# Seven block products in place of eight in the input projections of a two-layer encoder's feed-forwards

## The chip, the core and the metric

The kernel runs on one core of a Trainium2 chip. Its time is the device time of one execution in microseconds (us), and the figure for a kernel is the median of several executions. Engines are named as in the profile: PE multiplies matrices, PEld loads its weights, DVE, ACT and POOL are the vector, scalar and general engines, SP issues the DMAs.

## What is computed

A trunk of two layers runs over 576 tokens: a prompt of 512 and a sample of 64, which share all weights. Each layer is a feed-forward, a token mixer, and another feed-forward; so there are four feed-forwards. The change touches nothing but these. Cut to what matters, one is

```
def _swiglu(h, w_in, w_out):
    gate, up = jnp.split(h @ w_in, 2, axis=-1)      # w_in: 1024 x 5632
    return (jax.nn.silu(gate) * up) @ w_out         # w_out: 2816 x 1024

for l in range(DEPTH):                              # DEPTH = 2
    mod = (cond @ ada_w[l] + ada_b[l]).reshape(b, N_SUB, 3, D_MODEL)
    shift, scale, gate = mod[:, :, 0], mod[:, :, 1], mod[:, :, 2]
    hh = _modulated_norm(x, norm_g[l, 0], shift[:, 0], scale[:, 0])
    x = x + 0.5 * gate[:, 0, None] * _swiglu(hh, ff_w_in[l, 0], ff_w_out[l, 0])
    ...                                             # mixer, then the second feed-forward
```

Everything is float32. The vectors shift, scale and gate come from `cond @ ada_w`, nine products of 1024 x 1024 for each layer.

## The kernel before

**Layout.** Features lie in partitions, tokens along the free dimension. The 1024 features of the input are eight tiles of 128 (index k), and the tokens are two halves of 288. A float32 operand is held as two tiles in a rounded type: `XH`, the rounded value, and `XL`, what is left. A product of two operands is three matmuls (wh by XH, wh by XL, wl by XH), each a 128 x 128 weight against 288 columns, summed in one PSUM bank.

**Feed-forward** (`ffn`, line 638). The 2816 inner features are 22 column tiles. For each there is a pair of weight blocks, one of gate columns and one of up columns, each of eight 128 x 128 tiles (1024 columns in SBUF). `dense` (line 379) multiplies a pair: for each token half, gate over all k, then up over all k; 2 halves x 2 tiles x 8 k x 3 = 96 matmuls. After gate, ACT takes silu out of PSUM into `sg`; after up, DVE multiplies `sg` by the PSUM bank into `hm`, ACT rounds it into `HH`, DVE writes the rest into `HL`. The 22 tiles come in three chunks of 8, 8 and 6; after each chunk its share of the output projection is multiplied from `HH` and `HL` and added to the residual `x`. The first two pairs are multiplied together (`start_sub`, line 629; `dense_first`, line 431, in the first feed-forward), with their first token half running while the norm of the second half is still being worked out.

**Weights.** `w_dma` (line 354) fetches blocks of 512 KB by SP's queue into a ring of three buffers (`stage`). `w_prep` (line 364) splits one: ACT copies it rounded into `wh`, DVE subtracts that into `wl`; `wh` and `wl` are rings of four. During a pair the two blocks of the next pair are split.

**PSUM.** Two rings of four banks, `d` for the dense products and `a` for all else.

**Background work.** `ada_task` (line 585) works out shift, scale and gate on DVE while the feed-forwards run: for each of 136 weight tiles two operations of 1024 columns (`jk`). A planner (`Model`, `Sched`, lines 113 to 286) keeps rough times of each engine while the program is built, and puts a step of a background task into the instruction stream when its due time has come on PE's clock; the due times of `ada_task` are 5.6 us apart in the first feed-forward and 8.5 us in the next two. `finish` (line 278) builds a task to its end before anything else is built. The planner only sets the order in which instructions are written; each engine then works through its own list in that order.

All instructions are issued through one helper, so that nearly all rows carry line 188; operations are told apart by tile names.

Of the kernel before, what the change touches and what calls it, by code (L numbers as in the profile page):

```python
# [45 lines left out]
DSH = ((2, 4, 6), (1, 4, 6))  # L46


def plan():
    """The weight tiles in the order in which they are used, as pairs of blocks of up to eight 128 x 128 products;  # L50
    a tile is (source, index, rows, column)."""
# [6 lines left out]
    def ffn(f):  # L58
        for j0, nj in CHUNKS:
            for j in range(j0, j0 + nj):  # L60
                two([("in", f, tuple(range(8)), j * P), ("in", f, tuple(range(8)), FF + j * P)])
            ks = tuple(range(j0, j0 + nj))
            for ms in outs(nj):
                two([("out", f, ks, m * P) for m in ms])
# [40 lines left out]
def outs(nk):  # L105
    """The output tiles of each pair of blocks whose sums run over nk products."""
# [4 lines left out]
class Model:  # L111
    """Rough times of the engines, in ns, by which the background work is interleaved with the dense products."""
# [37 lines left out]
    def free(self, key, bufs):  # L150
        """When the ring's next buffer is free."""
# [73 lines left out]
class Ring:  # L225
    """A tile pool whose reuse of buffers the model sees."""
# [15 lines left out]
class Sched:  # L242
    """Interleaves the background work with the stream of dense products."""
# [45 lines left out]
def encoder_step(ctx: ExitStack, tc: tile.TileContext, a, o):  # L289
# [30 lines left out]
    # ---------------------------------------------------------------- constants  # L320
# [26 lines left out]
    # ---------------------------------------------------------------- weights  # L347
# [15 lines left out]

    def w_prep(i, g, E=None):
        if i >= len(pairs) or g >= len(pairs[i]):
            return
# [12 lines left out]
    def dense(evacs, ks=None, inter=False, mid=None):  # L379
        """The output tiles of a pair of blocks, or of two pairs, for the first half of the tokens, then for the  # L380
        second; evac(g, half, psum) for tile g of a pair."""
# [48 lines left out]

    def dense_first(evacs, feed):
        """The first two pairs of all, step by step for both halves as feed makes their inputs."""
# [36 lines left out]
    # ---------------------------------------------------------------- rsqrt, norms  # L469
# [23 lines left out]
    def norm_r(pool, halves):  # L493
        """1/rms of each token of these halves, tokens in partitions."""
# [61 lines left out]
    # ---------------------------------------------------------------- adaLN vectors  # L556
# [48 lines left out]
    # ---------------------------------------------------------------- the last products of a sub-layer  # L605
# [1022 lines left out]
```

## Time and profile before

| | |
|---|---|
| median of 3 runs | 2508.98 us (2506.79 to 2511.66) |
| profiled execution, first to last instruction | 2512.2 us; its time is listed as this span alone |
| PE busy | 2430.6 us, 97% |
| DVE busy | 1506.0 us, 60% |
| ACT busy | 835.3 us, 33% |
| POOL busy | 354.2 us, 14% |
| mean granted TensorE clock | 0.972 of full speed |

A row of the page's part 5 or of a grouped listing reads: line, engine, operation, output tile <- input tiles, shapes, count | busy us, mean ns of one | idle time of the engine before them and what ended it. PE's matmuls overlap, so their summed duration exceeds the span; the time that one takes from the stream is read from the chain of waits, which lists stretches of work with their number of instructions. A timeline row reads: start us, duration us, engine, line, operation, tiles, count, and in brackets how long the engine was idle before and who released it.

### The profile page before, as it was taken

The page shows a single profiled execution, that of the slowest core. Times are in us where ns is not written, and L with a number is a line of the kernel's source. Part 1 is how long each engine was busy: PE and PEld are TensorE (multiplying, and loading weights), DVE is VectorE, ACT ScalarE, POOL GpSimd, SP SyncE. Part 2 cuts the span into 40 slices and gives each one's busy share as a digit, 9 for nine tenths or more (in the row PEclk, how much of TensorE's full clock was granted, in tenths as well). Part 3 has the DMA queues.
Part 4 walks back from the last instruction along what each step waited for, and adds up shares of the span by engine and source line. Part 5 has one row for each costly group of instructions (what it writes and reads, how often), then busy time and mean ns, then how long its engine had stood idle before and what let it go on. Part 6 is the DMA issues. An engine that isn't in the chain of part 4 may idle for free.

```text
span 2512.2 us, 46274 instructions
## 1 busy us (share of the span) xinstructions
PE 2430.6 (97%) x19084; PEld 2357.9 (94%) x19084; DVE 1506.0 (60%) x2964; ACT 835.3 (33%) x1571; POOL 354.2 (14%) x599
## 2 busy tenths in 40 slices
PE   6999999999998999999999999999999999999998
PEld 5999999988888999999999999999888889999998
DVE  7677776597785666556556555535555664333334
ACT  4322212543322342122233222124655544222122
POOL 4000000341222220000021000002333332000001
PEclk8999999998877999999999999999999999999999
DMA  6555554321213144444434444322322122322222
GB/s 240 168 162 167 166 165 131 112 75 50 57 46 98 56 154 143 134 136 144 130 105 135 142 129 141 110 76 85 100 74 84 53 73 91 85 77 84 85 78 70
DMA packets 95399, 277.04 MB, mean 110 GB/s; under 512 B 24738, under 2 KB 27042, under 8 KB 94804
## 3 DMA queue, kind: packets, MB, share of 16 engines
q1 hardware_dynamic: 95188, 274.07, 34.7%
q8 instruction: 151, 2.47, 0.4%
q14 instruction: 60, 0.49, 0.1%
HBM read 262.52 MB, written 11.51 MB: 109 GB/s over the span
## 4 chain that ended last, share of the span: by engine, by line
PE 83%; DVE 10%; issue 3%; ACT 3%; POOL 2%; DMA 0%; SPq 0%; DVEq 0%; ACTq 0%; POOLq 0%
PE d L188 75%; PE a L188 8%; DVE iz L188 1%; DVE hf L188 1%; DVE cp L188 1%; POOL XL L188 1%; DVE t2k L188 1%; DVE sg L188 1%; ACT wh L188 1%; DVE sy L188 1%; POOL sn L188 1%; DVE wl L188 1%; POOL sg L188 1%; DVE raw L188 0%; ACT hf L188 0%
## 5 line engine op out<-in xcount | busy, mean ns | idle before, releaser
L188 PE MATMUL d<-XH,wh 128*128 128x288 f32 x3888 | 1176.0, 302 | 17.5 <-ACT XH L188 8.6
L188 PE MATMUL d<-XL,wh 128*128 128x288 f32 x3888 | 1158.9, 298 | 11.4 <-POOL XL L188 9.2
L188 PE MATMUL d<-XH,wl 128*128 128x288 f32 x3888 | 1155.7, 297 | 0.0
L188 PEld LDWEIGHTS d<-XH,wh 128*128 128x128 f32 x3888 | 739.3, 190 | 25.9 <-ACT XH L188 14.2
L188 PEld LDWEIGHTS d<-XL,wh 128*128 128x128 f32 x3888 | 740.1, 190 | 22.7 <-POOL XL L188 14.7
L188 PEld LDWEIGHTS d<-XH,wl 128*128 128x128 f32 x3888 | 739.6, 190 | 0.3
L188 DVE TENSOR_TENSOR wl<-stage,wh 128x1024 fp32r<-128x1024 f32 (+2 forms) x319 | 378.3, 1190 | 151.3 <-ACT wh L188 149.7
L188 ACT ACTIVATE wh<-stage 128x1024 fp32r<-128x1024 f32 (+2 forms) x345 | 348.8, 1019 | 321.1 <-PE d L188 255.1
L188 PE MATMUL d<-HH,wh 128*128 128x288 f32 x1408 | 416.3, 296 | 0.0
L188 PE MATMUL d<-HL,wh 128*128 128x288 f32 x1408 | 415.6, 295 | 0.0
L188 PE MATMUL d<-HH,wl 128*128 128x288 f32 x1408 | 414.1, 294 | 0.0
L188 DVE SCALAR_TENSOR_TENSOR jk<-aw,cb 128x1024 bf16<-128x1024 f32 x272 | 339.0, 1246 | 4.8
L188 POOL TENSOR_TENSOR acc<-acc,sq 128x288 f32<-128x288 f32 x72 | 58.7, 815 | 1613.0 <-ACT sq L188 1600.7
L188 DVE SCALAR_TENSOR_TENSOR x<-d,mod,x 128x64 f32<-128x64 f32 (+2 forms) x384 | 147.0, 412 | 220.2 <-PE d L188 218.7
L188 DVE TENSOR_TENSOR hm<-sg,d 128x288 f32<-128x288 f32 x174 | 78.9, 454 | 332.0 <-PE d L188 326.4
L188 PEld LDWEIGHTS d<-HH,wl 128*128 128x128 f32 x1408 | 264.5, 188 | 0.0
L188 PEld LDWEIGHTS d<-HL,wh 128*128 128x128 f32 x1408 | 264.2, 188 | 0.0
L188 PEld LDWEIGHTS d<-HH,wh 128*128 128x128 f32 x1408 | 264.1, 188 | 0.0
L188 ACT ACTIVATE HH<-hm 128x288 fp32r<-128x288 f32 x176 | 78.2, 444 | 545.3 <-DVE hm L188 545.3
L188 ACT ACTIVATE sg<-d 128x288 f32<-128x288 f32 x174 | 71.5, 411 | 248.1 <-PE d L188 247.8
L188 DVE TENSOR_TENSOR HL<-hm,HH 128x288 fp32r<-128x288 f32 x176 | 81.0, 460 | 90.3 <-ACT HH L188 90.3
L188 POOL TENSOR_TENSOR XL<-hf,XH 128x288 fp32r<-128x288 f32 x96 | 91.2, 964 | 83.8 <-ACT XH L188 82.9
(294 smaller groups left out, 1785.1 us busy)
## 6 DMA issues: line engine op xcount, KB each, us to landing
stage<-in_w SPq DMA_DIRECT2D x301, 512.0 KB, 3.7
aw<-in_ada SPq DMA_DIRECT2D x136, 512.0 KB, 3.5
stage<-in_w SPq DMA_DIRECT2D x36, 384.0 KB, 3.1
stage<-in_w SPq DMA_DIRECT2D x8, 320.0 KB, 2.8
x<-in_x SPq DMA_DIRECT2D x4, 576.0 KB, 7.0
xd<-x SPq DMA_DIRECT2D x1, 2304.0 KB
x<-xd SPq DMA_DIRECT2D x1, 2304.0 KB
out_k<-kf SPq DMA_DIRECT2D x8, 288.0 KB, 3.9
```

The lines of the kernel that those rows point to most:

```text
L188: r = real(*args, **kw)
```

## The change

20 of the 22 pairs of each feed-forward (all but the first two) are multiplied as 2 x 2 blocks. The blocks of the weights are gate or up columns against even or odd k; those of the input are even or odd k against the first or second token half. Seven products of blocks, each of 4 k x 3 = 12 matmuls, give what eight gave (`dense7`). Four of the seven take sums of weight blocks or of input blocks as operands. The input's sums (`TH`, `TL`) are made once for each feed-forward by a new task `t_task`, built between the first two pairs and the third; the weights' sums are made for every pair on POOL (`w_sum`), and four `wh`/`wl` tiles are split for a pair in place of two (`w_tile`). The seven products go into three PSUM banks: P1, P6, P7 and P4 one after the other into the same one, which is read in between, P5 and P3 into another, P2 into a third. `evac7` reads them. Weight blocks of these pairs are stored with their even k first. A few buffers of the prologue move into the new tile's place, and 512 bytes are set as the size of a DMA scratch buffer. Comments and docstrings go. The core of the diff (blank lines left out):

```
+PLAIN = 2
+EVEN_ODD = (0, 2, 4, 6, 1, 3, 5, 7)
...
-                two([("in", f, tuple(range(8)), j * P), ("in", f, tuple(range(8)), FF + j * P)])
+                ks = tuple(range(8)) if j < PLAIN else EVEN_ODD
+                two([("in", f, ks, j * P), ("in", f, ks, FF + j * P)])
...
+    def seven(i):
+        return i < len(pairs) and pairs[i][0][0][2] == EVEN_ODD
+    ss = {}
+    spool = [None]
+    HB = 4 * P
+    def w_split(i, src, E=V):
+        n = Model.size(src)
+        h, l = wsp.tile([P, 1024], F32R, name="wh"), wsp.tile([P, 1024], F32R, name="wl")
+        wt.setdefault(i, []).append((h, l))
+        for c in range(0, n, HB):
+            A.activation(h[:, c:c + HB], src[:, c:c + HB], AF.Copy)
+        E.tensor_sub(l[:, :n], src, h[:, :n].bitcast(F32))
+    def w_sum(i, n):
+        g0, g1 = st[i, 0], st[i, 1]
+        a11, a12, a21, a22 = g0[:, :HB], g0[:, HB:], g1[:, :HB], g1[:, HB:]
+        if n in (1, 3):
+            ss[i, n] = spool[0].tile([P, 1024], F32, name="ss", bufs=2)
+        x1, x2 = ss[i, 1], ss.get((i, 3))
+        if n == 1:
+            G.tensor_add(x1[:, HB:], a21, a22)
+        if n == 2:
+            G.tensor_sub(x1[:, :HB], x1[:, HB:], a11)
+        if n == 3:
+            G.tensor_sub(x2[:, :HB], a11, a21)
+        if n == 4:
+            G.tensor_sub(x2[:, HB:], a12, x1[:, :HB])
+    def w_tile(i, n):
+        if n == 0:
+            w_split(i, st[i, 0])
+        if n == 1:
+            w_split(i, ss[i, 1])
+        if n == 2:
+            w_split(i, ss.pop((i, 3)))
+            ss.pop((i, 1))
+            st.pop((i, 0))
+            w_dma()
+        if n == 3:
+            w_split(i, st[i, 1][:, HB:])
+            st.pop((i, 1))
+            w_dma()
     def w_prep(i, g, E=None):
         if i >= len(pairs) or g >= len(pairs[i]):
+            return
+        if seven(i):
+            if g == 0:
+                w_sum(i, 1)
+                w_tile(i, 0)
+                w_sum(i, 2)
+            else:
+                w_sum(i, 3)
+                w_tile(i, 1)
             return
...
+    TH, TL = {}, {}
+    def dense7(evac):
+        i = pos[0]
+        pos[0] += 1
+        nxt7 = seven(i + 1)
+        h0, h1 = slice(0, 288), slice(288, 576)
+        x11 = lambda k: (XH[:, 2 * k, h0], XL[:, 2 * k, h0])
+        x21 = lambda k: (XH[:, 2 * k + 1, h0], XL[:, 2 * k + 1, h0])
+        x22 = lambda k: (XH[:, 2 * k + 1, h1], XL[:, 2 * k + 1, h1])
+        t = lambda n: lambda k: (TH[0][:, n - 1, k], TL[0][:, n - 1, k])
+        order = (("P1", 0, x11), ("P2", 0, x21), ("P6", 1, t(2)), ("P5", 1, t(1)), ("P7", 2, t(3)), ("P3", 2, x22),
+                 ("P4", 3, t(4)))
+        bank = {}
+        for n, (name, u, xf) in enumerate(order):
+            b = {"P2": "b", "P5": "c", "P3": "c"}.get(name, "a")
+            if b not in bank:
+                bank[b] = psum.tile([P, 288], F32, name="d")
+            wh, wl = wt[i][u]
+            c0 = HB if name in ("P2", "P5", "P3") else 0
+            for k in range(4):
+                c = c0 + k * P
+                H, L = xf(k)
+                f, e = k == 0 and name in ("P1", "P2", "P5"), k == 3
+                kw = {"skip_group_check": True}
+                T.matmul(bank[b], wh[:, c:c + P], H, start=f, stop=False, **kw)
+                T.matmul(bank[b], wh[:, c:c + P], L, start=False, stop=False, **kw)
+                T.matmul(bank[b], wl[:, c:c + P], H, start=False, stop=e, **kw)
+                S.tick()
+            evac(name, bank[b])
+            if n == 0:
+                while len(wt[i]) < 4:
+                    if len(wt[i]) == 2:
+                        w_sum(i, 4)
+                    w_tile(i, len(wt[i]))
+            if nxt7:
+                if n in (1, 2, 3, 4):
+                    w_sum(i + 1, n)
+                if n in (2, 4, 6):
+                    w_tile(i + 1, n // 2 - 1)
+            elif n in (2, 4):
+                w_prep(i + 1, n // 2 - 1)
+        wt.pop(i)
+    def t_task(pool):
+        TH[0] = pool.tile([P, 4, 4, 288], F32R, name="TH")
+        TL[0] = pool.tile([P, 4, 4, 288], F32R, name="TL")
+        h0, h1 = slice(0, 288), slice(288, 576)
+        Hf, Lf = XH.bitcast(F32), XL.bitcast(F32)
+        def parts(n, k, t, E):
+            A.activation(TH[0][:, n - 1, k], t, AF.Copy)
+            E.tensor_sub(TL[0][:, n - 1, k], t, TH[0][:, n - 1, k].bitcast(F32))
+        new = lambda: npool.tile([P, 288], F32, name="hf", bufs=5)
+        for k in range(4):
+            e, o = 2 * k, 2 * k + 1
+            t1, b = new(), new()
+            G.tensor_sub(t1, Hf[:, e, h1], Hf[:, e, h0])
+            G.tensor_sub(b, Lf[:, e, h1], Lf[:, e, h0])
+            V.tensor_add(t1, t1, b)
+            t2 = new()
+            V.tensor_sub(t2, Hf[:, o, h1], t1)
+            V.tensor_add(t2, t2, Lf[:, o, h1])
+            yield S.clock + 300.0
+            parts(2, k, t2, V)
+            parts(1, k, t1, G)
+            t3, d = new(), new()
+            G.tensor_sub(t3, Hf[:, o, h1], Hf[:, e, h1])
+            G.tensor_sub(d, Lf[:, o, h1], Lf[:, e, h1])
+            V.tensor_sub(t2, Hf[:, o, h0], t2)
+            V.tensor_add(t2, t2, Lf[:, o, h0])
+            yield S.clock + 300.0
+            V.tensor_add(t3, t3, d)
+            parts(3, k, t3, V)
+            parts(4, k, t2, G)
+            yield S.clock + 300.0
...
+        spool[0] = pool
+        tt = None
+        def evac7(jj):
+            g, up = {}, {}
+            def put(half, h):
+                t0, t1 = HALF[half]
+                A.activation(HH[:, jj, t0:t1], h, AF.Copy)
+                return lambda: V.tensor_sub(HL[:, jj, t0:t1], h, HH[:, jj, t0:t1].bitcast(F32))
+            def evac(step, ps):
+                if step == "P1":
+                    g[0] = pool.tile([P, 288], F32, name="sg", bufs=2)
+                    A.activation(g[0], ps, AF.Copy)
+                if step == "P2":
+                    V.tensor_add(g[0], g[0], ps)
+                    A.activation(g[0], g[0], AF.Silu)
+                if step == "P6":
+                    g[1] = pool.tile([P, 288], F32, name="sg", bufs=2)
+                    A.activation(g[1], ps, AF.Copy)
+                if step == "P5":
+                    up[0] = pool.tile([P, 288], F32, name="p5")
+                    A.activation(up[0], ps, AF.Copy)
+                if step == "P7":
+                    up[1] = pool.tile([P, 288], F32, name="up")
+                    A.activation(up[1], ps, AF.Copy)
+                    G.tensor_add(up[1], up[1], up[0])
+                if step == "P3":
+                    V.tensor_add(g[1], g[1], ps)
+                    A.activation(g[1], g[1], AF.Silu)
+                if step == "P4":
+                    h1, h0 = (pool.tile([P, 288], F32, name="hm", bufs=2) for _ in range(2))
+                    V.tensor_mul(h1, g[1], up[1])
+                    f1 = put(1, h1)
+                    V.tensor_mul(h0, g[0], ps)
+                    f1()
+                    put(0, h0)()
+            return evac
         for ci, (j0, nj) in enumerate(CHUNKS):
...
+                    tt = S.spawn(t_task(pool))
+                elif seven(pos[0]):
+                    if tt:
+                        S.finish(tt)
+                        tt = None
+                    dense7(evac7(jj))
...
-        crow = [ap.tile([P, D], F32, name="awp", bufs=3)[0:1] for _ in range(2)]
+        first = fp.tile([P, 4, 4, 288], F32, name="TH").rearrange("p a b c -> p (a b c)")
+        crow = [first[0:1, g * D:(g + 1) * D] for g in range(2)]
...
-        row = ap.tile([P, D], F32, name="awp", bufs=3)[:, :P]
+        row = first[:, 2 * D:2 * D + P]
...
-                w = w[ks[0] * P:(ks[-1] + 1) * P]
-                tiles.append(w.reshape(len(ks), P, P).transpose(1, 0, 2))
+                w = w[:(max(ks) + 1) * P].reshape(-1, P, P)[list(ks)]
+                tiles.append(w.transpose(1, 0, 2))
...
-    nc = _bacc.Bacc("TRN2", target_bir_lowering=False, num_devices=1)
+    nc = _bacc.Bacc("TRN2", target_bir_lowering=False, num_devices=1, dynamic_dma_scratch_size=512)
```

## Rows read from the trace of the kernel before

**Rows 1.** The page, part 4: the chain that ended last, by line.

```profile
PE d L188 75%; PE a L188 8%; DVE iz L188 1%; DVE hf L188 1%; DVE cp L188 1%; POOL XL L188 1%; DVE t2k L188 1%; DVE sg L188 1%; ACT wh L188 1%; DVE sy L188 1%; POOL sn L188 1%; DVE wl L188 1%; POOL sg L188 1%; DVE raw L188 0%; ACT hf L188 0%
```

**Rows 2.** The chain in order of time: start us, us, what, number of instructions.

```profile
61.85 1.59 PE d L188 x12
...
71.82 386.68 PE d L188 x2916
...
2094.94 395.43 PE d L188 x2981
```

**Rows 3.** Busy time by stretch, first and last feed-forward; span, PE, PEld, DVE, ACT, POOL, clock, DMA.

```profile
71.00:461.00 390.00, 389.59 (x2945) 389.35 (x2944) 273.95 (x460) 101.64 (x163) 7.27 (x9) 1.00 0.51 160
...
2094.00:2492.00 398.00, 397.94 (x3005) 397.66 (x3006) 138.94 (x219) 103.40 (x164) 9.63 (x12) 1.00 0.27 79
```

**Rows 4.** ACT's operations by form: count | busy us, mean ns | idle before.

```profile
L188 ACT ACTIVATE wh<-stage 128x1024 fp32r<-128x1024 f32 x301 | 313.5, 1049 | 317.2 <-PE d L188 251.2 <-issue 53.7 <-DVE jk L188 8.6
L188 ACT ACTIVATE HH<-hm 128x288 fp32r<-128x288 f32 x176 | 78.2, 444 | 545.3 <-DVE hm L188 545.3
L188 ACT ACTIVATE sg<-d 128x288 f32<-128x288 f32 x174 | 71.5, 411 | 248.1 <-PE d L188 247.8
...
L188 ACT ACTIVATE cH<-ck 128x512 fp32r<-128x512 f32 x8 | 5.1, 632 | 2.2 <-DMA ck<-in_ck 2.0
```

**Rows 5.** DVE's operations by form.

```profile
L188 DVE SCALAR_TENSOR_TENSOR jk<-aw,cb 128x1024 bf16<-128x1024 f32 x272 | 339.0, 1246 | 4.8
L188 DVE TENSOR_TENSOR wl<-stage,wh 128x1024 fp32r<-128x1024 f32 x275 | 337.1, 1229 | 127.3 <-ACT wh L188 125.7 <-POOL XL L188 1.6
L188 DVE TENSOR_TENSOR HL<-hm,HH 128x288 fp32r<-128x288 f32 x176 | 81.0, 460 | 90.3 <-ACT HH L188 90.3
L188 DVE TENSOR_TENSOR hm<-sg,d 128x288 f32<-128x288 f32 x174 | 78.9, 454 | 332.0 <-PE d L188 326.4 <-ACT sg L188 4.7 <-ACT XH L188 0.8
```

**Rows 6.** Timeline of DVE, then of ACT, in the third feed-forward.

```profile
1483.29 0.45 DVE L188 TENSOR_TENSOR hm<-sg,d 128x288 f32<-128x288 f32 x1 [3.19 <-PE d L188]
1484.26 0.46 DVE L188 TENSOR_TENSOR HL<-hm,HH 128x288 fp32r<-128x288 f32 x1 [0.51 <-ACT HH L188]
1485.20 1.23 DVE L188 TENSOR_TENSOR wl<-stage,wh 128x1024 fp32r<-128x1024 f32 x1 [0.49 <-ACT wh L188]
1486.35 1.22 DVE L188 SCALAR_TENSOR_TENSOR jk<-aw,cb 128x1024 bf16<-128x1024 f32 x1
...
1483.78 0.45 ACT L188 ACTIVATE HH<-hm 128x288 fp32r<-128x288 f32 x1 [3.31 <-DVE hm L188]
1484.13 1.04 ACT L188 ACTIVATE wh<-stage 128x1024 fp32r<-128x1024 f32 x1
```

**Rows 7.** POOL's operations by form.

```profile
L188 POOL TENSOR_TENSOR wl<-stage,wh 128x1024 fp32r<-128x1024 f32 x26 | 64.0, 2465 | 150.8 <-ACT wh L188 119.7 <-issue 24.6 <-PE d L188 6.5
L188 POOL TENSOR_TENSOR acc<-acc,sq 128x288 f32<-128x288 f32 x72 | 58.7, 815 | 1613.0 <-ACT sq L188 1600.7 <-issue 11.8
```

**Rows 8.** Timeline of POOL and DVE at 628 us, then of DVE, POOL and PE at 902 us.

```profile
628.05 2.40 POOL L188 TENSOR_TENSOR wl<-stage,wh 128x1024 fp32r<-128x1024 f32 x1 [5.68 <-issue]
628.24 2.84 DVE L188 SCALAR_TENSOR_TENSOR x<-raw,small,x 128x579 f32<-128x579 f32 x1
...
901.63 1.21 DVE L188 SCALAR_TENSOR_TENSOR jk<-aw,cb 128x1024 bf16<-128x1024 f32 x1
901.71 3.50 POOL L188 TENSOR_TENSOR XL<-hf,XH 128x288 fp32r<-128x288 f32 x2 [0.61 <-ACT XH L188]
902.88 1.69 DVE L188 SCALAR_TENSOR_TENSOR jk<-aw,cb 128x1024 bf16<-128x1024 f32 x1
903.54 0.40 PE L188 MATMUL d<-XL,wh 128*128 128x288 f32 x1 [1.31 <-POOL XL L188]
```

**Rows 9.** Busy time and clock by stretch around 906 us; columns as in Rows 3.

```profile
902.00:904.00 2.00, 0.69 (x5) 0.46 (x5) 1.97 (x3) 0.71 (x3) 2.00 (x2) 1.00 0.00 0
...
906.00:908.00 2.00, 2.00 (x11) 2.00 (x10) 0.91 (x2) 1.40 (x3) 0.00 (x0) 0.50 0.00 0
```

## The prediction, made before the changed kernel was run

> **What bounds the kernel now.** Read the chain of waits by line first: three quarters of the span is PE's dense matmuls [rows 1]. In order of time the feed-forwards stand out as unbroken runs of 387 to 395 us each [rows 2], and the busy time by stretch agrees: PE is busy for 390 of 390 us in the first and 398 of 398 in the last, at full clock [rows 3]. In these stretches nothing but the number of matmuls counts: 395.43 us for 2981 is 0.1326 us each [rows 2]. DVE is busy 274 us of 390 in the first feed-forward, where the `ada_task` runs, and 139 of 398 in the last, where it doesn't; ACT some 102, POOL 7 to 10 [rows 3]. All these have slack now, so the question is whether they still have it when PE needs less and they get more.
>
> **What PE saves.** A pair falls from 96 to 84 matmuls: 12.73 to 11.14 us. Over 80 pairs that is 960 matmuls, **-127 us**. It is had only if PE is kept fed.
>
> **What each pair adds elsewhere.** Splits: four tiles in place of two; on DVE 1.23 us each, and on ACT two halves of 512 columns, at the 0.63 us of `cH` [rows 4, 5]. Reading the banks: ACT has eight operations of 0.41 to 0.44 us where it had four, DVE six of 0.45 where it had four [rows 4, 5]. POOL: four sums of 512 columns and one of 288. The 288 take 0.80, 1024 took 2.40 undisturbed, so 512 should take about 1.29; 6.0 us a pair [rows 7, 8]. Totals per pair: ACT 8.5, DVE 7.6, POOL 6.0, each under 11.14. By busy time alone PE stays the bound. Two things speak against it.
>
> **The first is the order of the lists.** P1, P6, P7 and P4 share a bank, so P7 can't start until ACT has copied P6 out, and ACT and DVE work strictly down their lists. Follow one turn, starting at DVE's add for P2. Behind an operation of another engine I count its duration and 0.04 us; behind one of the same engine 0.08 to 0.10 less, since they overlap (`HH` to `wh` is 0.35 us from start to start, `wl` to `jk` 1.15) [rows 6]:
> add P2 0.49; ACT silu 0.33; ACT copy of P6, in the list behind that silu, 0.47; P7 on PE 1.90 (12 matmuls are 1.59 [rows 2], the rest is start and drain); ACT copy of P7 0.33; ACT halves of tile 1 1.20; DVE `wl` 1.15; DVE add P3, behind it, 0.49; ACT silu 0.45; DVE first product `hm` 0.49; ACT two `HH` 0.74; ACT tile 2 1.06; ACT copy of the next P1 0.33; ACT tile 3 1.20; DVE `wl` 1.15; and behind that the next pair's add P2.
> The sum is **11.8 us**, a closed ring that no engine can shorten: already 0.6 more than PE's 11.14.
>
> **The second is that POOL and DVE take turns.** Where both read two SBUF tensors, one waits: at 902 us two `XL` on POOL, 0.80 each alone, take 3.50 while a `jk` on DVE grows from 1.21 to 1.69; at 628 us a DVE operation ends 0.6 us after the POOL one that it started under, having taken 2.84 [rows 8]. Before the change POOL has 7 to 10 us of work in a feed-forward [rows 3]; after it, some 140 more. Where the sums fall in the ring: once P7 is copied, POOL starts the 0.80 us addition and then sum 4, which holds until about 0.9 us after `wl` of tile 1 is ready; sum 1 of the next pair may start when that `wl` is done (same buffer) and makes the first `hm` wait 0.4; sum 3 may start when `wl` of tile 2 is done, within 0.1 us of when `wl` of tile 3 is ready, and costs 1.0 or nothing. So 11.8 + 0.9 + 0.4 + (0 to 1.0) = 13.1 to 14.1; I take **13.6 us**, above the 12.73 of before. In place of -127 us the 80 pairs then cost 80 x 0.87 = **+70**. Ends: 11.14 (-127) if all of this overlaps, 14.6 (+150) if the clock also falls at times.
> The Trainium skill has this as a rule ("SBUF — State Buffer", section "SBUF: two separate sides"): the port pair that the two engines share is an exclusive lock, held for a whole instruction. That this case's trace shows, with the 2.84 above, though the hand-over hides some 0.2 us (an `XL` costs 0.6 there, not 0.80). By the rule to the letter, port time alone would be 4.9 + 1.4 on DVE and 6.0 on POOL, 12.3 us a pair, and the most to be saved over 80 pairs 35 us. The sum here stands without it.
>
> **`ada_task`.** A step of it is two `jk`, 2.4 us of DVE, now in DVE's idle time [rows 5, 6]. 128 steps run in or around the first three feed-forwards (136 less the eight of the prologue); the twenty pairs are 0.61 of a feed-forward (20 x 12.73 of some 420 us), so 78 fall among them. Put between add P2 and `wl` of tile 0 one costs nothing, since DVE waits there; before add P2, before add P3 or before `hm`, the whole 2.4. Of the seven steps of a pair three are such, two cost most of it or less. A floor is DVE's and POOL's shared time: with two and a half in a pair, as the planner will have it in the first feed-forward, DVE's list is 12.9 us (7.6 less its overlaps, and 6.0 of `jk`) and POOL's part that can't lie beside it some 4, 16.8 against 14.1, so 1.1 each. I take 1.1: **+86 us**; ends 0 and 2.0 (+156).
>
> **`t_task`.** This is the surest cost. It is built to its end between the first two pairs and the third (`finish` stands before the first `dense7`). Its DVE and ACT operations so lie behind the last `hm`, `HH` and `HL` of pair two, which end 1.4 us after PE's last matmul of it [rows 6], and ahead of ACT's copy of P1, which P6 needs. PE has P1 and P2 to do, 3.3 us, then nothing. How long is the task? Per k, in a chain: POOL two subtractions 1.6; DVE three operations, 1.2; ACT two 288-column roundings 0.8; POOL one subtraction 0.8, POOL two more, with DVE between them taking turns, 1.9; DVE add 0.5; ACT two roundings 0.8; POOL subtraction 0.8, and 0.05 at each hand-over: 8.5 us. Only POOL's first two can run early. Four k are 33 us; PE idles 30. After idling PE restarts at half clock: it did when the stalls around 902 us were over (granted 0.50 in the two us from 906, 11 matmuls where full clock has 15) [rows 9]; two to four us of that cost 1 to 2. The first pair then waits for sum 4, behind the task on POOL, and an `ada` step may stand in the task. I take 32 us, four times: **+128**. Ends: POOL's 24 operations alone, 19 us, less what PE does meanwhile, 15 (+60); 40 (+160).
>
> **Chunk ends.** Both halves of `HH` and `HL` now come after P4, where the first half came a half-pair earlier. The output projection needs the last of them 21 matmuls in, 2.8 us; the ring lets it have them some 3.5 to 4 us after P4. 1 us x 12 = **+12** (0 to 20).
>
> **Weights and prologue.** The same bytes, and an SP queue that has a whole pair for two blocks: nothing, as DMA is busy a half of the time or less [rows 3]. The moved buffers of the prologue are free when `TH` needs them: nothing.
>
> **The sum**: +70 + 86 + 128 + 12 = +296 us. The span read was 2512.2, 3 us above the median of the runs; 2509 + 296 = **2805 us**.
>
> **Rivals.**
> *POOL does not hold DVE up* (its sums fall into DVE's gaps). For it: DVE has 3.5 us of gaps in a pair; against it: rows 8. Then 11.8 us a pair, -74; `ada` 0.6 each, +47; `t_task` 31 x 4 = +124; ends +12: 2618 us.
> *Faster.* The place is the copy of P6: if DVE reaches add P2 and ACT the silu before P5 ends, PE never waits in a pair, -127, `ada` lies in the gaps, 0, and `t_task` goes at POOL's own pace, 17 x 4 = +68: 2450 us. It decides from `t_task` under 32 us per feed-forward and pairs at 11.14. For it: every engine's total is under 11.14; against it: the ring of 11.8, which holds without any waiting for POOL.
> *The stalls feed on the clock.* PE would idle a fifth of each pair in pieces of one to two us; around 902 us such pieces brought the clock down [rows 9]. Then 14.6 a pair, +150; `ada` 2.0, +156; `t_task` 38 x 4 = +152; ends +20: 2987 us.
> *Nothing gained or lost*: the pairs gain what `t_task` costs, 2509.
>
> **How the numbers follow.** The forecast 0.56, POOL alongside 0.18, the clock 0.14, faster 0.09, level 0.03. The range is 2590 to 2950: the forecast's own ends, the first rival, and the lower part of the clock's. A measurement of this kernel can tell 0.2% (5 us) from no change; faster by more than that 0.09, within it 0.03, slower 0.88.
>
> **What would show it.** In the profile after: PE with four idle stretches of about 30 us, each near the start of a feed-forward, with POOL and DVE alternating under them; in the last feed-forward a turn from P1 to the next P1 of 13 to 14 us, with PE's waits put down to ACT's copies out of `d`; `wl` on DVE well above 1.23 us in the mean, POOL busy some 900 us in place of 354; and a longer turn where `jk` runs. It is wrong if PE runs through the pairs at 0.133 us a matmul, if the gap before the third pair is under 15 us, or if `wl` keeps its duration beside POOL's sums.

## The result: 2867 us, 14% slower, and the profile after

The changed kernel takes 2867.23 us (median of 4, 2850.6 to 2869.0) where the kernel before took 2509.9 (median of 4): ratio 1.1409, 95% interval 1.1379 to 1.1438. The profiled execution has a span of 2866.0 us, 353.8 more than before. The forecast was 2805, so the direction and the range held; of its terms two were badly sized, with opposite signs. (Executions of the kernel before take some 2494 or some 2509 us, a difference that lies in the mixer and that later variants show as well, so medians or stretches of a trace are compared below, not single spans.)

The page of the changed kernel, PE's row of part 1 and both rows of part 4:

```profile
PE 2414.1 (84%) x18124; PEld 2312.4 (81%) x18124; DVE 1960.3 (68%) x3412; ACT 1105.6 (39%) x2355; POOL 1057.5 (37%) x1095
...
PE 49%; DVE 25%; ACT 12%; issue 10%; POOL 4%; DMA 0%; DVEq 0%; ACTq 0%; SPq 0%; POOLq 0%
PE d L191 42%; DVE wl L191 8%; PE a L191 7%; DVE jk L191 5%; ACT wh L191 5%; ACT sg L191 3%; DVE sg L191 2%; DVE hf L191 2%; POOL hf L191 2%; DVE hm L191 2%; DVE iz L191 1%; ACT HH L191 1%; POOL TL L191 1%; ACT TH L191 1%; DVE cp L191 1%
```

The dense matmuls were 75% of the chain [rows 1] and are 42%; DVE and ACT had 13% of it (part 4 of the page before: `PE 83%; DVE 10%; issue 3%; ACT 3%`) and have 37%. The unbroken runs of 387 to 395 us [rows 2] are gone. By stretch (columns as in [rows 3]), the changed kernel's first and last feed-forward:

```profile
71.00:506.00 435.00, 328.38 (x2175) 320.98 (x2176) 344.61 (x486) 136.70 (x291) 172.42 (x108) 0.87 0.36 124
...
2430.00:2850.00 420.00, 366.88 (x2703) 360.32 (x2704) 233.65 (x327) 165.09 (x348) 163.64 (x126) 0.96 0.24 75
```

PE was busy in all of both [rows 3]; now it idles 107 us in the first and 53 in the last, and the mean granted clock is down to 0.87 and 0.96. POOL has 172 and 164 us where it had 7 to 10. DVE's and POOL's forms in the changed kernel (count | busy us, mean ns | idle before):

```profile
L191 DVE SCALAR_TENSOR_TENSOR jk<-aw,cb 128x1024 bf16<-128x1024 f32 x272 | 403.9, 1485 | 4.8
L191 DVE TENSOR_TENSOR wl<-ss,wh 128x1024 fp32r<-128x1024 f32 x160 | 263.3, 1645 | 124.9 <-ACT wh L191 96.5 <-PE d L191 21.4 <-issue 3.1
...
L191 DVE TENSOR_TENSOR sg<-sg,d 128x288 f32<-128x288 f32 x160 | 71.1, 444 | 0.0
...
L191 DVE TENSOR_TENSOR hm<-sg,up 128x288 f32<-128x288 f32 x80 | 45.6, 570 | 42.7 <-ACT sg L191 42.7
```

```profile
L191 POOL TENSOR_TENSOR ss<-stage 128x512 f32<-128x512 f32 x160 | 253.6, 1585 | 642.2 <-DMA stage<-in_w 473.6 <-DVE wl L191 93.3 <-DVE HL L191 51.5
L191 POOL TENSOR_TENSOR ss<-ss,stage 128x512 f32<-128x512 f32 x80 | 147.3, 1841 | 6.3
```

`jk` and the `wl` of the sums read two SBUF tensors and take 1485 and 1645 ns in the mean, where `jk` and `wl` took 1246 and 1229 before [rows 5]. `sg<-sg,d`, which reads one of its two from PSUM, takes 444, where `hm<-sg,d` took 454 before [rows 5]. That is the turn-taking of [rows 8], all through the feed-forwards.

**A pair without `ada_task`.** I measure a turn from one `hm<-sg,up` to the next; before, it was 12.73 us. In the last feed-forward it has two steady lengths: 11.82 us in the first chunk, 13.4 to 13.8 in the other two. Timeline of PE, ACT and DVE in a turn of 11.82 us:

```profile
2473.53 0.40 PE L191 MATMUL d<-TH,wh 128*128 128x288 f32 x1 [2.07 <-ACT sg L191]
...
2485.35 0.40 PE L191 MATMUL d<-TH,wh 128*128 128x288 f32 x1 [0.42 <-ACT sg L191]
...
2478.60 0.41 ACT L191 ACTIVATE up<-d 128x288 f32<-128x288 f32 x1 [1.08 <-PE d L191]
2478.91 1.14 ACT L191 ACTIVATE wh<-ss 128x512 fp32r<-128x512 f32 x2
...
2482.05 0.44 ACT L191 ACTIVATE sg<-sg 128x288 f32<-128x288 f32 x1 [2.00 <-DVE sg L191]
2483.15 0.81 ACT L191 ACTIVATE HH<-hm 128x288 fp32r<-128x288 f32 x2 [0.66 <-DVE hm L191]
2483.87 1.13 ACT L191 ACTIVATE wh<-ss 128x512 fp32r<-128x512 f32 x2
2484.91 0.39 ACT L191 ACTIVATE sg<-d 128x288 f32<-128x288 f32 x1
...
2480.14 1.51 DVE L191 TENSOR_TENSOR wl<-ss,wh 128x1024 fp32r<-128x1024 f32 x1 [1.49 <-ACT wh L191]
2481.57 0.44 DVE L191 TENSOR_TENSOR sg<-sg,d 128x288 f32<-128x288 f32 x1
2482.60 0.52 DVE L191 TENSOR_TENSOR hm<-sg,up 128x288 f32<-128x288 f32 x1 [0.58 <-ACT sg L191]
...
2485.03 1.23 DVE L191 TENSOR_TENSOR wl<-ss,wh 128x1024 fp32r<-128x1024 f32 x1 [0.58 <-ACT wh L191]
2486.18 0.68 DVE L191 TENSOR_TENSOR wl<-stage,wh 128x512 fp32r<-128x512 f32 x1
```

Read it by time (tiles 0 to 3 are the four that `w_tile` splits for a pair, sums 1 to 4 those of `w_sum`). PE starts P6 at 2473.53 and does P6, P5 and P7; ACT copies P7 at 2478.60 and splits tile 1 at 2478.91; DVE's `wl` of it starts at 2480.14, the add for P3 stands behind it at 2481.57; then silu (2482.05), `hm` (2482.60), `HH` (2483.15), tile 2 (2483.87), and only behind these the copy of the next P1 (2484.91), which the next P6 (2485.35) waits for. A closed ring of 11.82 us, in which PE idles 0.7. In a turn of 13.4 us the same engines look like this (POOL and DVE; the last row is POOL in the turn of 11.82):

```profile
2649.30 1.27 POOL L191 TENSOR_TENSOR ss<-stage 128x512 f32<-128x512 f32 x1 [3.93 <-DVE HL L191]
2650.65 2.16 POOL L191 TENSOR_TENSOR ss<-ss,stage 128x512 f32<-128x512 f32 x1
...
2649.77 1.88 DVE L191 TENSOR_TENSOR wl<-ss,wh 128x1024 fp32r<-128x1024 f32 x1 [0.57 <-ACT wh L191]
2651.58 1.77 DVE L191 TENSOR_TENSOR wl<-stage,wh 128x512 fp32r<-128x512 f32 x1
...
2486.43 1.57 POOL L191 TENSOR_TENSOR ss<-stage 128x512 f32<-128x512 f32 x1 [3.63 <-DMA stage<-in_w]
```

Here sum 1 starts 0.5 us ahead of `wl` of tile 2, and the two sums stretch both `wl` to 1.88 and 1.77. In the turn of 11.82 us sum 1 has to wait for its block until 2486.43, after these `wl` have begun (2485.03 and 2486.18); they take 1.23 and 0.68. What sum 1 waited for doesn't tell the two lengths apart: a turn earlier, in the fast chunk, it starts at 2474.49 behind a `wl`, and in the slow chunk it waits for its DMA too in two turns (2608.95 and 2622.32) and still comes ahead of the `wl`.

**A pair with `ada_task`.** Timeline of DVE, POOL and PE in the first feed-forward:

```profile
169.92 2.31 DVE L191 SCALAR_TENSOR_TENSOR jk<-aw,cb 128x1024 bf16<-128x1024 f32 x1
...
172.28 2.17 DVE L191 SCALAR_TENSOR_TENSOR jk<-aw,cb 128x1024 bf16<-128x1024 f32 x1
...
174.38 0.44 DVE L191 TENSOR_TENSOR sg<-sg,d 128x288 f32<-128x288 f32 x1
...
169.59 1.56 POOL L191 TENSOR_TENSOR ss<-stage 128x512 f32<-128x512 f32 x1 [3.67 <-DMA stage<-in_w]
171.23 2.13 POOL L191 TENSOR_TENSOR ss<-ss,stage 128x512 f32<-128x512 f32 x1
173.33 2.25 POOL L191 TENSOR_TENSOR ss<-stage 128x512 f32<-128x512 f32 x1
...
175.65 0.61 PE L191 MATMUL d<-TH,wh 128*128 128x288 f32 x1 [3.12 <-ACT sg L191]
```

A step's two `jk` stand between `wl` of tile 3 and the add for P2 (174.38), which P7 waits for through ACT. They meet three sums on POOL and take 4.46 us where they take 2.4 alone; PE has nothing for 3.12 us and comes back at half clock (columns of [rows 3]; PE's count is 22 in the five us at 0.50, 39 in five at 1.00):

```profile
176.00:181.00 5.00, 5.00 (x22) 5.00 (x22) 4.13 (x6) 2.38 (x6) 1.58 (x2) 0.50 0.48 192
182.00:187.00 5.00, 5.00 (x39) 5.00 (x39) 3.69 (x8) 3.11 (x7) 1.19 (x1) 1.00 0.49 172
```

The Trainium skill ("SBUF — State Buffer", section "SBUF: two separate sides") says that the port pair is an exclusive lock, held for a whole instruction. The trace agrees but for 0.3 us that overlap: three sums and two `jk` one after the other would be 3 x 1.27 + 2 x 1.22 = 6.3 us, and they took 5.99 (169.59 to 175.58). And the one that comes first keeps its time: the sum at 2649.30 takes 1.27, the `wl` that starts 0.47 us behind it 1.88 in place of 1.23.

**`t_task`.** PE has four gaps, of 35.9, 32.1, 32.0 and 31.2 us, each in the third pair, ahead of its P6. Timeline of DVE and PE in the last:

```profile
2433.57 0.46 DVE L191 TENSOR_TENSOR hf<-hf 128x288 f32<-128x288 f32 x1 [2.24 <-POOL hf L191]
...
2442.32 0.46 DVE L191 TENSOR_TENSOR hf<-hf 128x288 f32<-128x288 f32 x1 [2.24 <-POOL hf L191]
...
2457.76 0.61 PE L191 MATMUL d<-TH,wh 128*128 128x288 f32 x1 [31.19 <-ACT sg L191]
```

One k takes 8.75 us (2433.57 to 2442.32). After the gap the granted clock is 0.50 in the window 2458 to 2461 us; 15 matmuls take 3.8 us where full clock needs 2.0, 1.8 us more.

### The profile page after: what moved, and what is told of

The parts are those of the page before. It is cut to its first block, busy times and chain, and to the rows that moved or that the text cites. A ratio compares the mean times of both kernels' runs of the same rounds, so it can differ in the third digit from the quotient of the medians.

```text
span 2866.0 us, 46285 instructions
## 1 busy us (share of the span) xinstructions
PE 2414.1 (84%) x18124; PEld 2312.4 (81%) x18124; DVE 1960.3 (68%) x3412; ACT 1105.6 (39%) x2355; POOL 1057.5 (37%) x1095
## 4 chain that ended last, share of the span: by engine, by line
PE 49%; DVE 25%; ACT 12%; issue 10%; POOL 4%; DMA 0%; DVEq 0%; ACTq 0%; SPq 0%; POOLq 0%
PE d L191 42%; DVE wl L191 8%; PE a L191 7%; DVE jk L191 5%; ACT wh L191 5%; ACT sg L191 3%; DVE sg L191 2%; DVE hf L191 2%; POOL hf L191 2%; DVE hm L191 2%; DVE iz L191 1%; ACT HH L191 1%; POOL TL L191 1%; ACT TH L191 1%; DVE cp L191 1%
## 5 line engine op out<-in xcount | busy, mean ns | idle before, releaser
L191 PE MATMUL d<-XH,wh 128*128 128x288 f32 x2288 | 715.6, 313 | 14.2 <-ACT XH L191 8.6
L191 PE MATMUL d<-TH,wh 128*128 128x288 f32 x1280 | 417.6, 326 | 364.4 <-ACT sg L191 364.4
L191 PE MATMUL d<-XL,wh 128*128 128x288 f32 x2288 | 696.5, 304 | 11.0 <-POOL XL L191 8.6
L191 PE MATMUL d<-XH,wl 128*128 128x288 f32 x2288 | 691.6, 302 | 0.0
L191 DVE TENSOR_TENSOR wl<-stage,wh 128x1024 fp32r<-128x1024 f32 (+3 forms) x319 | 374.8, 1178 | 227.9 <-ACT wh L191 226.3
L191 POOL TENSOR_TENSOR ss<-stage 128x512 f32<-128x512 f32 x160 | 253.6, 1585 | 642.2 <-DMA stage<-in_w 473.6
L191 PEld LDWEIGHTS d<-XL,wh 128*128 128x128 f32 x2288 | 449.8, 197 | 18.1 <-POOL XL L191 14.5
L191 PEld LDWEIGHTS d<-XH,wl 128*128 128x128 f32 x2288 | 447.9, 196 | 0.1
L191 ACT ACTIVATE wh<-stage 128x512 fp32r<-128x512 f32 (+3 forms) x425 | 322.8, 784 | 228.7 <-PE d L191 205.9
L191 DVE SCALAR_TENSOR_TENSOR jk<-aw,cb 128x1024 bf16<-128x1024 f32 x272 | 403.9, 1485 | 4.8
L191 PE MATMUL d<-TL,wh 128*128 128x288 f32 x1280 | 403.7, 315 | 0.0
L191 PE MATMUL d<-TH,wl 128*128 128x288 f32 x1280 | 402.4, 314 | 0.0
L191 DVE TENSOR_TENSOR wl<-ss,wh 128x1024 fp32r<-128x1024 f32 x160 | 263.3, 1645 | 124.9 <-ACT wh L191 96.5
```

The costliest lines, as they stand in the source:

```text
L191: r = real(*args, **kw)
```

## The experiments

Each is told with its median and its ratio to runs of the kernel before on the same chip. Where an experiment is said to take less than the changed kernel, that is less than 2867.23; the kernel before had medians of 2509.4 to 2511.6 beside the experiments and 2509.9 beside the changed kernel, so some 2 us of such a difference can be the chips'. A diff is against the changed kernel unless it says otherwise.

**POOL's weight sums left out** (the splits read unsummed blocks).

```
     def w_sum(i, n):
+        return
...
-            w_split(i, ss[i, 1])
+            w_split(i, st[i, 1])
...
-            w_split(i, ss.pop((i, 3)))
-            ss.pop((i, 1))
+            w_split(i, st[i, 0])
```

> The changed kernel with the four weight sums of each pair left out (tiles 1 and 2 are split from the unsummed blocks), so POOL has 1 operation a pair in place of 5. Theory A (turn-taking of POOL and DVE stretches what stands in the lists): wl and jk fall back to 1.23 us in the mean, pairs of the last feed-forward from 11.8 to 13.6 us down to 11.2 to 11.6, pairs with ada steps from 15 to 18 down to 13 to 14; in all some 220 us less, 2645 us. Rival B (the pairs lose by PE's half clock after its gaps, gaps that come from the lists alone): the gaps stay, under 60 us less, over 2800.

2692.52 us, ratio 1.073 (1.0689 to 1.0771): 175 us less, where 222 were expected. Its DVE forms:

```profile
L191 DVE TENSOR_TENSOR wl<-stage,wh 128x1024 fp32r<-128x1024 f32 x355 | 435.8, 1230 | 307.3 <-ACT wh L191 304.4 <-POOL XL L191 1.6 <-PE d L191 1.2
L191 DVE SCALAR_TENSOR_TENSOR jk<-aw,cb 128x1024 bf16<-128x1024 f32 x272 | 350.3, 1288 | 4.8
```

`wl` is back at 1230 ns and every pair without `ada` takes 11.4 us, in all chunks alike: the whole of 13.4 less 11.4 is the sums, and rival B, with its under 60 us, is out. Even without the sums the lists hold a pair above PE's 11.14. What was missed: with two `ada` steps a pair still takes 15.0, which is 1.8 a step without any sum on POOL. This run also shows that it is the place that costs, at one step a pair; DVE in two pairs of the second feed-forward:

```profile
1056.23 0.45 DVE L191 TENSOR_TENSOR hm<-sg,up 128x288 f32<-128x288 f32 x1
...
1063.16 1.22 DVE L191 TENSOR_TENSOR wl<-stage,wh 128x1024 fp32r<-128x1024 f32 x1 [2.38 <-ACT wh L191]
1064.31 1.22 DVE L191 SCALAR_TENSOR_TENSOR jk<-aw,cb 128x1024 bf16<-128x1024 f32 x1
...
1069.48 0.46 DVE L191 TENSOR_TENSOR hm<-sg,up 128x288 f32<-128x288 f32 x1 [0.58 <-ACT sg L191]
...
1085.33 0.46 DVE L191 TENSOR_TENSOR hm<-sg,up 128x288 f32<-128x288 f32 x1 [0.58 <-ACT sg L191]
...
1089.45 0.45 DVE L191 TENSOR_TENSOR sg<-sg,d 128x288 f32<-128x288 f32 x1
1089.81 1.22 DVE L191 SCALAR_TENSOR_TENSOR jk<-aw,cb 128x1024 bf16<-128x1024 f32 x1
...
1096.74 0.46 DVE L191 TENSOR_TENSOR hm<-sg,up 128x288 f32<-128x288 f32 x1 [0.58 <-ACT sg L191]
```

In the first the step's two `jk` stand behind the `wl` of tile 0 and ahead of that of tile 1, and the turn is 13.25 us; in the second they stand behind the add for P2, and it is 11.41, as without a step.

**The `jk` of `ada_task` left out** (its DMAs stay; `mod` is a constant).

```
-                ada_tile(pool, cb, l, j, kt)
+                aw.pop((l, j * 8 + kt))
+                if kt == 0:
+                    V.memset(mod[:, l, j], 0.1)
```

> The changed kernel with the two jk of every ada step left out (shift, scale and gate are a constant; the weights are still fetched). Theory A: the ada steps cost some 200 us and not the 86 forecast, because they stand in DVE's list ahead of the add of P2; without them the pairs of the first three feed-forwards take what those of the last take, 11.8 to 13.6 us: 2665 us. Rival C (weights or their sums arrive late, POOL waits 474 us for stage): the pairs stay at 15 to 18, 2800 or more.

2659.84 us, ratio 1.0591 (1.054 to 1.0641): 207 us less than the changed kernel, 5 more than expected. Between the first and the last turn of the feed-forwards 187 us went (77, 72, 37 and 1 by feed-forward); 176 of them in the 68 turns that hold no chunk's end, with 75 steps: 2.3 us a step. These turns now average 12.91 us in a mix of 11.4, 11.8 and 13.4. This prices two terms at once: `ada` +207, the pairs by themselves 80 x (12.91 - 12.73) = +14. Rival C is out: POOL's sums still wait 396 us for `stage` in this run (474 in the changed kernel), and yet the pairs fall to 12.91. A part of the 2.3 is the clock: in the 68 turns of the changed kernel PE is busy 139 us at a granted clock of 0.50, which costs 70 us at most, and here 10 us, which cost 5.

**Splits of tiles 2 and 3 moved behind the copies, the sums one product later.**

```
-                while len(wt[i]) < 4:
-                    if len(wt[i]) == 2:
-                        w_sum(i, 4)
-                    w_tile(i, len(wt[i]))
+                if (i, 4) not in done4:
+                    w_sum(i, 4)
+                w_tile(i, 2)
+            if n == 2:
+                w_tile(i, 3)
...
-                if n in (1, 2, 3, 4):
-                    w_sum(i + 1, n)
+                if n in (2, 3, 4, 5):
+                    w_sum(i + 1, n - 1)
```

> The changed kernel with the splits of tiles 2 and 3 moved in the lists: tile 2 behind ACT's copy of the next P1, tile 3 behind the copy of P6, the sums one step later. Same work. Theory A (PE waits for copies that stand behind splits in ACT's and DVE's lists): pairs of the last feed-forward 11.2 to 11.6 us in place of 11.8 to 13.6, and the ada pairs shorter by 2 to 4; 2740 us. Rival B or C: 2867 within 20 us.

2839.45 us, ratio 1.1312 (1.1267 to 1.1357): 28 us less, where 127 were expected. In the last feed-forward the turns of the two slow chunks fall from 13.4 to 12.1 us; those of the first chunk are 10.9, 13.8, 11.2, 11.8 and 11.1, in the mean no less than the 11.82 of before. So this run doesn't show that the copy of P1 behind tile 2 closes the ring of 11.82, which is read from the rows of the changed kernel; it shows that other rings lie near. Most pairs with `ada` stay at 14 to 21. The chain of waits of this kernel in the last feed-forward:

```profile
2585.63 3.72 POOL ss L191 x2
...
2589.36 3.47 DMA stage<-in_w
...
2594.38 1.61 POOL ss L191
2595.99 1.75 POOL up L191
2597.74 3.71 POOL ss L191 x2
```

The later sums free the weight buffer later, its DMA lands 3.5 us after, and the next sum waits for that: here POOL and the queue are what the chain goes through.

**`t_task` spread over three more plain pairs.**

```
-PLAIN = 2
+PLAIN = 5
...
-            yield S.clock + 300.0
+            yield S.clock + 2800.0
```

> The changed kernel with five plain pairs per feed-forward in place of two, and the steps of t_task 2.8 us apart on the planner's clock, so that it is built into the plain pairs. Theory A: the four gaps of 31 to 36 us go (about 132 us), and three pairs more at the plain 12.73 us save another 30 where ada runs: 2705 us. Rival: its operations hold up the plain pairs' own in the lists and half of the gap comes back there: 2770 us.

2751.86 us, ratio 1.096 (1.0919 to 1.1001): 115 us less, where 162 were expected. The gaps ahead of the first P6 shrink from 131.2 us to 8.4, 4.9, 4.9 and 5.0, so they were the task. Twelve pairs are plain now, too, and the task's own operations hold some of them up: in the waits, `PE d <- DVE hm` has 17.4 us in four waits of up to 5.2. What is left of the gaps and these waits come to 41 us, near the 47 missed; that they are the cause was not tried.

**`ada` let into a pair only during P6**, behind the add for P2, in the second and third feed-forward (due times 6.5 us).

```
+                hold[0] = n != 2 and late[0]
                 S.tick()
+                hold[0] = False
...
-        at = S.spawn(ada_task(ap, cb, [(1, j) for j in range(9)], 8500.0))
+        late[0] = True
+        at = S.spawn(ada_task(ap, cb, [(1, j) for j in range(9)], 6500.0))
```

> The changed kernel with the ada steps of the second and third feed-forward let into a seven-product pair only while P6 is multiplied, so that they stand in DVE's list between the add of P2 and the split of tile 0, where DVE waits anyway (their due times 6.5 us apart in place of 8.5, so that all find room); the first feed-forward as it was. Theory A (it is the place in the list that costs): the pairs of those two fall from 16.5 and 15.2 us in the mean to 13.4 to 14.2, 85 us less in all, 2783 us. Rival (a step costs DVE's time wherever it stands): about 16 us still, 2850 or more.

2768.63 us, ratio 1.1037 (1.1011 to 1.1063): 99 us less, 14 more than expected. DVE in a pair of the second feed-forward:

```profile
1094.23 0.45 DVE L191 TENSOR_TENSOR sg<-sg,d 128x288 f32<-128x288 f32 x1
1094.59 1.96 DVE L191 SCALAR_TENSOR_TENSOR jk<-aw,cb 128x1024 bf16<-128x1024 f32 x1
...
1096.59 2.20 DVE L191 SCALAR_TENSOR_TENSOR jk<-aw,cb 128x1024 bf16<-128x1024 f32 x1
```

The `jk` still take turns with POOL (1.96 and 2.20), but they stand behind the add for P2, and a pair with one takes 13.7 us beside 13.4 without: 0.3 a step in place of 2.3. By the 34 turns of these two feed-forwards, against those of the run without `jk`, it is 11 us for 29 steps, 0.4. The edit also leaves at most one step in a pair, where the changed kernel has one or two, and moves 12 of 41 steps out of these turns; so by itself it doesn't part place from crowding. The run without sums does, with one step a pair (11.41 and 13.25): the price of `ada` is for the most part its place. The first feed-forward, where nothing was changed, stays at 15 to 21 us.

**Seven products for every other pair, from the eighth on**, so that a plain pair can take up what the other leaves; late splits as above, sum 4 behind sum 3 in `w_prep`, and `t_task` spread over the plain pairs.

```
-PLAIN = 2
+PLAIN = 7
...
+                ks = EVEN_ODD if j >= PLAIN and j % 2 and f in (0, 1, 2, 3) else tuple(range(8))
...
+                w_sum(i, 4)
...
+            yield S.clock + 4500.0
```

> Seven products for every other pair from the eighth on (8 of 22 in each feed-forward), so that POOL has two pairs' time for one pair's sums; splits of tiles 2 and 3 later in the lists; t_task spread over the five plain pairs before, 4.5 us a step. Theory A (ring and turn-taking): a seven-product pair takes 11.1 to 11.4 us, a plain one 12.73 still, 8 x 1.4 = 11 us gained in the last feed-forward, about 10 in the second and third, nothing or a loss of 10 in the first, where ada is dense: 2485 us against 2512. Rival: the sums and t_task hold up the plain pairs' evacuations instead, no gain, 2512 or more.

2537.93 us, ratio 1.011 (1.0087 to 1.0132), 53 us above what was expected. In the last feed-forward two pairs take 23.9 us, which is 96 + 84 matmuls at 0.1326, without a gap. With four `ada` steps in two pairs, as in the first, they take 28.2 to 29.5.

**The same, with the first feed-forward plain**: `f in (1, 2, 3)`.

> The kernel e6_alternate with the first feed-forward left plain, as before the change. Theory A: 2480 us, since the ada steps of the first leave no room there. Rival: as e6_alternate, 2512 or more.

2510.06 us, ratio 0.999 (0.9967 to 1.0012): no gain, and 30 us above what was expected. Two pairs with three `ada` steps still take 26.7 to 28.6. The plain pairs lose as well: from the last matmul of the second feed-forward to the first output projection of the third, where all pairs but one are plain and `t_task` is spread among them, the trace has 121.7 us, where the kernel before has 109.0.

**With `ada` only during P6 as well** (the edit of the place, on the last one).

> e7_alternate_not0 with the ada steps let into a seven-product pair only while P6 is multiplied (due times 6.5 us apart). Theory A: what e7 gave back in the second and third feed-forward (two pairs 26.7 to 28.6 us with ada, 23.9 without) comes from steps in bad places; with this 24 to 25 us, 2485 us. Rival: DVE and POOL together are full there whatever the place, 26 to 28 us still, 2510.

2517.66 us, ratio 1.0016 (0.999 to 1.0043), 33 us above what was expected. Two pairs with three steps take 24.8 to 25.1, so the place works, but the steps crowd into the plain first pairs beside `t_task`, and it is lost there: the stretch of 109.0 us before takes 125.9.

**Seven products in the last feed-forward alone**, where there is no `ada`: `f in (3,)`, eight pairs in all.

> e7_alternate_not0 with seven products in the last feed-forward alone, where no ada runs: 8 pairs x 1.59 us = 12.7 us less than before the change, 2498 us, ratio 0.995. Rival: some of it comes back at the end of the run, 2505 or more.

2496.67 us (12 runs), ratio 0.9949 (0.9925 to 0.9972), as expected: 0.5% faster than the kernel before. Its chain has the last feed-forward in one run:

```profile
2076.18 382.74 PE d L191 x2885
```

Before it was 395.43 us and 2981 matmuls [rows 2]: 12.69 us less for 8 x 12 matmuls, 0.132 each, all that there was to be had; and `t_task` cost nothing there. The other feed-forwards' runs have the lengths of before (386.68, 395.35 and 393.79), and the stretch ahead of the third one's first output projection is 109.0 us again, with the same due times of `ada` as in the run of 121.7 but without `t_task`.

**Alternate pairs in three feed-forwards, with no `ada` in them** (held for the span of these pairs, due times 4.3 us elsewhere).

> e7_alternate_not0 with no ada step in the alternating pairs at all; their due times are 4.3 us apart in the plain first pairs and the output projections of the second and third feed-forward. Theory A: all 24 seven-product pairs gain 1.59 us, 38 us, less what the denser ada and t_task cost the first pairs, about 12: 2485 us. Rival: the steps fill DVE in the output projections and cost there what they cost in the pairs: 2510.

2506.28 us, ratio 0.9983 (0.996 to 1.0007), 21 us above what was expected. All alternating pairs run at 23.9 us for two, but in the second and third feed-forward the unbroken run is only 270.93 and 275.47 us long: the first pairs, with `ada` closer together and `t_task`, lose what the others gain (the stretch of 109.0 us takes 124.5).

## Why the prediction was right, and where it was not

The terms, in us, beside what the runs gave:

| term | forecast | measured | from |
|---|---|---|---|
| pairs without `ada` | +70 | +14 | 12.91 a turn with the `jk` left out |
| `ada_task` | +86 | +207 | median with the `jk` left out |
| `t_task` | +128 | +138 | four gaps, 131.2, and 1.8 each at half clock |
| chunk ends | +12 | 0 | below |
| sum | +296 | +359 | the profiled execution: +354 |

- **PE's saving is had only if PE is fed: right.** At alternate pairs without `ada` it is had to the last matmul (12.69 us of 12.7), at 20 pairs in a row in the mean not at all (12.91 a turn without `ada`; only the turns of 11.82 keep 0.9 of the 1.59).
- **The ring through the lists: the kind right, the path wrong.** The text closed it through the add for P2, with a tile 3 of two ACT halves (1.20) and a `wl` of 1.15. Tile 3 has half the columns (0.62 and 0.68 in the trace), so that path is 1.1 us shorter (the same full width stands in the port time of 4.9 on DVE). The ring that closes goes through the copy of the next P1 behind tile 2, and that it comes to 11.82 as well is luck. In it the `wl` of tile 1 takes 1.51, already stretched by a sum, where the text's ring held without any waiting for POOL. That it is the lists and not totals is shown by the run without sums: 11.4, still over 11.14.
- **POOL and DVE take turns: right, at 0.4 (turns of 11.82) to 2.0 (turns of 13.4) over the 11.4 without sums, in place of 1.3 to 2.3.** Taking POOL's sums away gave 11.4 everywhere and `wl` at 1230 ns. The mean is less than the 13.6 taken because in part of the chunks sum 1 comes late enough to miss the two `wl` (11.8), and the other chunks settle at 13.4. POOL was busy 1057.5 us where some 900 were expected: its sums were stretched too (1585 to 1841 ns in the mean in place of 1.29 us). The rival in which POOL does not hold DVE up is refuted by the same run.
- **`ada_task`: the step that failed.** 1.1 a step was a count of DVE's and POOL's port time. It measured 2.3, and another 31 us went with the steps outside these turns, at chunk ends and in the first pairs (some of that may have been there before the change). The price comes mostly from order: a step in front of an add, or of a split that the add stands behind, delays ACT's copy and by it PE; this costs 1.8 a step even without sums, the step of 2.4 us grows to 4.46 beside them, and P7 then runs at half clock (at most 70 of the 176 us that went in the turns). The text had said that before add P2 it costs the whole, but then averaged over places; of the 75 steps in the turns the planner put only 9 into the free place between the add for P2 and tile 0. The run with steps only there shows it: 0.3. Even the upper end given, 2.0, was too low.
- **`t_task`: right.** 8.75 us per k against 8.5, gaps of 31 to 36 against 30, restart at half clock 1.8 after the last gap (taken for all four) against 1 to 2. Spreading it took most of the gaps away.
- **Chunk ends: nothing.** PE does wait for `HH` at four places, 4.2 us in all, but the turn as a whole isn't longer: without `ada` the one across a chunk's end is 63.1 us; the 384 matmuls of the output projection in it take 50.9 at 0.1326, which leaves 12.2, less than a turn of before.
- **The rival of the clock** named a real part. Half clock follows the gaps of 3 to 5 us that `ada` makes in the first three feed-forwards, up to 70 us by the figures above; in the last, without `ada`, there is none after `t_task` (the 0.96 is of a stretch that holds its gap), though PE idles for 0.4 to 1.0 us at a time in every turn.

So that the forecast came within 62 us is luck: +121 on `ada` stood against -56 on the pairs. The 5 us by which the measured terms exceed the trace's own difference are not assigned.

## What to carry to other kernels

When a change moves work from a saturated engine to idle ones, totals by engine don't decide; write out one turn as a closed ring through every engine's list, with each tile at its real width, and look for a copy or an add that stands behind a long operation. Background work that was free while another engine was the bound has a price by its place: put it behind the instruction that the bound engine waits for, not in front. A saving that overloads the helpers in every iteration can be had in every other one, as the eight alternating pairs of the last feed-forward showed (0.9949), but only where the helpers have the room: with `ada` about, the same in three feed-forwards gained nothing (0.999).

## What was not expected of the hardware

- The same instruction stream settles at two lengths, 11.82 and 13.4 us a turn, and stays in one for a whole chunk. They differ by whether POOL's first sum starts before or after two `wl` on DVE. What puts a chunk into the one or the other was not tried.
- Taking turns for the port shows on both engines: sums of 1.27 us alone average 1.59 to 1.84, `jk` reaches 2.31 and a `wl` of 512 columns 1.77 (0.68 alone), while DVE's operations with one operand in PSUM stay at 444 to 446 ns.
- After the gap of 3.12 us PE ran five us at its level of 1.2 GHz (granted 0.50); the turns of 11.82 us, with 0.7 us of idling in each, ran at 2.4 GHz throughout (granted 1.00).
